# Linear attention with its gate terms made early and kept in DRAM, its halves pipelined in software, the second values projection moved last, and the first scores' operands loaded by another queue

## The chip, the cores and the metric

The kernel runs on one core of one Trainium2 chip. The metric is the device time of one execution in microseconds (us). The engines are named as in the profile: PE is the matmul engine, PEld its weight loads, DVE the vector engine, ACT the scalar engine, POOL the GpSimd engine, SP the engine that here only issues DMAs. A queue named SPq or ACTq is the stream of DMA issues on that engine.

## What is computed

One encoder block for 1024 tokens of width 1024. The part that the change touches is the pair of token mixers, fed by one projection of `x`:

```python
proj = h @ w_in[l]
aq, ak, av, iq, ik, iw, bq, bk, bv, br, bg = jnp.split(proj, split_points, axis=-1)
ya = dsa_mixer(aq, ak, av, iq, ik, iw)          # index scores -> top 256 keys per query -> softmax attention
log_a = log_sigmoid(bg @ w_gla_gate + b_gla_gate) / 16
ob = gla_mixer(bq, bk, bv, log_a)               # chunks of 64 tokens
```
and within `gla_mixer`
```python
b = jnp.cumsum(log_a, axis=2)                   # inside a chunk
qg = qf * jnp.exp(b);  kg = kf * jnp.exp(-b)
A = where(causal, qg @ kg.T, 0);  o_intra = A @ v
kd = kf * jnp.exp(b_last - b);  kv = kd.T @ v;  decay = exp(b_last)
S_next = decay * S + kv;  o_inter = qg @ S_prev
```
Then `mix = [ya | yb] @ w_out`, a layer norm, a mixture of 32 experts with two chosen per token, and a second layer norm.

## The kernel before

`run` opens with `in_phase`: index projections (`index_queries`, `index_keys`), half of the first values projection (`values(0, ...)`), then `index_scores`, which for six query tiles of 128 rows makes eight score products each and, between them, draws steps from a generator `rest`. `rest_inputs` (line 448) makes that generator: first the second values projection, `values(1, ...)`, then `gla_inputs`, which for each of two head pairs projects queries and keys, values, and the output gate of the linear attention and stores them in DRAM (`d_gqk`, `d_gv`, `d_gr`). What is left of `rest` runs after the scores. Then come `queries_keys` (the attention's queries and keys, four weight pieces, rotated by DVE and POOL, stored to `d_q` and `d_k`), `topk_phase` (a threshold search bit by bit over 31 bits, by counting on DVE for four row tiles and on ACT for two, then a tail of six tiles that makes the bias), and `gla_phase` with high priority.

`gla_phase` loops over two head pairs and two halves of the tokens. `gla_half` (line 540) loads its operands, makes the gate terms (lines 553 to 572: four matmuls, a log-sigmoid out of Exp and Ln on ACT, four cumulative-sum matmuls, two Exp), then `kd` by transposes, the masked products, the chunk states `S` one after the other on DVE, the outputs, their norm, and four transposes for each head whose copy `ym` is stored to `d_mix`.

The `attention` works through 32 items, four head pairs by eight query tiles, in an order written out by hand on PE, ACT and DVE (`manual_schedule`). Everything before it is ordered by the framework's planner, which fixes each engine's stream ahead of time: an engine runs its stream in order and stands at an instruction whose operand is not there. `attention_loads(0, ...)` (line 328) loads the operands of the first head pair into the pool `first_qk`, which takes the memory of the linear attention's pool; its values go into a buffer of the pool `big`, whose buffers hold the split `x` while projections run. Inside the attention, `rb` (line 875), the spread reciprocals of the softmax sums, is made by POOL and read by PE in `shares`; `split_wout` (line 904) also works on POOL.

After the attention come the output projection (line 997), the router and the experts (line 1208), whose weights stream in by DMA.

## Time and profile before

| | |
|---|---|
| median of 3 runs | 1330.31 us (1326.86 to 1330.82) |
| the profiled execution | 1329.53 us |
| its span, first to last instruction | 1327.7 us |
| PE busy over the span | 92% |
| DVE, ACT, POOL busy | 78%, 61%, 29% |

The profiled execution lies 0.8 us under the median. Its 1.8 us outside the span are what surrounds the first and last instruction. The busy shares are means over stages that have different limits: up to 124 us the index scores, from there to 392 us the top-k search beside projections and linear attention, to 415 us the last projections, from 428 to 554 us the attention, then the output projection and the router, and from 700 us the experts.

### The profile page before, as it was taken

The numbers are of one execution on the slowest core, as the hardware profiler recorded it, in microseconds if no ns is written. First come the engines' busy times: TensorE is split into PE (matmuls) and PEld (weight loads), VectorE is DVE, ScalarE is ACT, GpSimd is POOL, SyncE is SP. The second block draws the span as 40 slices with busy tenths as digits, with TensorE's granted clock in tenths as the row PEclk, the third lists the DMA queues.
The fourth block names the chain that finished last, engine by engine and source line by source line (L and its number), as shares of the span: only waits on it lengthen the run. The fifth ranks groups of instructions, "written<-read, shape, count | busy, mean of one in ns | idle before, by whom it ended". The sixth has DMA issues, their size and how long they took to land.

```text
span 1327.7 us, 19294 instructions
## 1 busy us (share of the span) xinstructions
PE 1219.5 (92%) x6894; PEld 1013.7 (76%) x6894; DVE 1032.4 (78%) x1647; ACT 803.9 (61%) x1120; POOL 385.3 (29%) x340
## 2 busy tenths in 40 slices
PE   6999999999886899999959999999999999999952
PEld 5986987987665778778857888888888888888741
DVE  4378799899882556467677899999999999998945
ACT  4366577676321666422146777787777787777735
POOL 2412633234763245011120222122112222212014
PEclk9999999999898999999969999999999999999985
DMA  7643334223325793387366999999999999999926
GB/s 251 169 127 114 120 97 134 97 82 106 100 65 176 227 268 96 117 311 273 124 218 257 361 364 378 380 376 361 372 362 369 352 363 357 346 355 343 331 40 253
DMA packets 127652, 318.51 MB, mean 240 GB/s; under 512 B 15353, under 2 KB 45842, under 8 KB 127554
## 3 DMA queue, kind: packets, MB, share of 16 engines
q1 hardware_dynamic: 114754, 287.86, 61.3%
q0 software_dynamic: 10496, 21.00, 6.1%
q10 hardware_dynamic: 2304, 8.39, 1.6%
q8 instruction: 55, 0.90, 0.3%
q14 instruction: 43, 0.35, 0.1%
HBM read 281.74 MB, written 52.23 MB: 252 GB/s over the span
## 4 chain that ended last, share of the span: by engine, by line
PE 63%; DMA 12%; DVE 12%; ACT 5%; issue 4%; POOL 2%; SPq 1%; POOLq 0%; ACTq 0%; DVEq 0%
PE acc L1208 24%; PE ot L1208 11%; PE acc L997 6%; PE acc L235 4%; DMA big<-we 3%; PE acc L221 3%; DVE gt L689 3%; PE pt L1271 3%; DMA d_y<-y,tok 2%; PE s L795 2%; PE ot L833 2%; PE pt L819 2%; PE g L235 2%; DMA d_mix<-ym 1%; ACT jnk L719 1%
## 5 line engine op out<-in xcount | busy, mean ns | idle before, releaser
L180 DVE TENSOR_TENSOR elo<-big,ehi 128x2048 fp32r<-128x2048 f32 (+1 forms) x132 | 268.2, 2060 | 24.6 <-ACT ehi L179 22.1
L179 ACT CAST ehi<-big 128x2048 fp32r<-128x2048 f32 (+1 forms) x132 | 223.3, 1725 | 7.8 <-DMA big<-we 3.6
L1208 PE MATMUL acc<-ehi,xh 128*128 128x512 f32 x512 | 206.4, 403 | 2.0 <-ACT sg L1320 2.0
L1208 PE MATMUL acc<-ehi,xl 128*128 128x512 f32 x512 | 203.4, 397 | 2.5 <-DVE xl L180 2.5
L1208 PE MATMUL acc<-elo,xh 128*128 128x512 f32 x512 | 203.1, 397 | 1.2 <-DVE elo L180 1.2
L221 PE MATMUL acc<-big,whi 128*128 128x512 f32 (+1 forms) x432 | 137.5, 398 | 11.3 <-ACT big L179 10.8
L1278 POOL DMA_INDIRECT xg<-d_h,tok x32 | 37.0, 1157 | 366.8 <-PE pt L1271 366.0
L235 PE MATMUL acc<-whi,big 128*128 128x256 f32 x640 | 120.6, 287 | 0.0
L1257 POOL DMA_INDIRECT d_y<-y,tok x32 | 89.3, 2792 | 106.1 <-DVE y L1256 45.9
L1208 PEld LDWEIGHTS acc<-ehi,xl 128*128 128x128 f32 x512 | 97.0, 189 | 26.2 <-DVE xl L180 3.2
L1208 PEld LDWEIGHTS acc<-ehi,xh 128*128 128x128 f32 x512 | 97.2, 190 | 24.1 <-ACT sg L1320 2.5
L1208 PEld LDWEIGHTS acc<-elo,xh 128*128 128x128 f32 x512 | 97.3, 190 | 23.0 <-DVE elo L180 1.6
L221 PEld LDWEIGHTS acc<-big,whi 128*128 128x128 f32 x432 | 82.9, 196 | 29.2 <-ACT big L179 10.8
L1208 PE MATMUL ot<-ehi,ah 128*128 128x512 f32 x256 | 103.6, 405 | 0.9 <-ACT ah L179 0.9
L689 DVE TENSOR_SCALAR_CACHE_REDUCE gt<-sc,cand 128x384 bf16<-128x384 f32 (+1 forms) x124 | 100.4, 809 | 4.1 <-POOL sc L701 1.6
L180 DVE TENSOR_TENSOR elo<-slot,ehi 128x2048 fp32r<-128x2048 f32 (+1 forms) x46 | 95.5, 2100 | 9.5 <-ACT ehi L179 9.1
L235 PEld LDWEIGHTS acc<-whi,big 128*128 128x128 f32 x640 | 101.1, 192 | 1.8 <-issue 1.0
L1208 PE MATMUL ot<-ehi,al 128*128 128x512 f32 x256 | 101.1, 395 | 0.8 <-DVE al L180 0.8
L1208 PE MATMUL ot<-elo,ah 128*128 128x512 f32 x256 | 101.0, 394 | 0.0
L235 PE MATMUL acc<-wlo,big 128*128 128x256 f32 x320 | 91.9, 288 | 0.0
L719 ACT ACTIVATE jnk<-sc,cand 128x896 bf16<-128x896 f32 (+1 forms) x62 | 67.9, 1095 | 35.4 <-DVE cand L715 26.9
L997 PE MATMUL acc<-wohi,m 128*128 128x512 f32 x256 | 83.8, 402 | 2.4 <-ACT m L179 2.4
(287 smaller groups left out, 2616.7 us busy)
## 6 DMA issues: line engine op xcount, KB each, us to landing
big<-we SPq DMA_DIRECT2D x79, 1024.0 KB
big<-wf SPq DMA_DIRECT2D x40, 1024.0 KB
slot<-we SPq DMA_DIRECT2D x26, 1024.0 KB
sc<-we SPq DMA_DIRECT2D x20, 1024.0 KB
slot<-wf SPq DMA_DIRECT2D x16, 1024.0 KB
wraw<-wi SPq DMA_DIRECT2D x52, 256.0 KB
sc<-wf SPq DMA_DIRECT2D x8, 1024.0 KB
raw<-xT SPq DMA_DIRECT2D x8, 512.0 KB
```

Source lines behind the costliest of these rows:

```text
L179: nc.scalar.copy(hi, src)
L180: (lo_eng or nc.vector).tensor_tensor(lo, src, hi.bitcast(F32), op=OP.subtract)
L221: nc.tensor.matmul(ps[:m, :n], l[:, j, c0:c0 + m], r[:, j % 2, t0:t0 + n], start=(j == 0 and a == 0), stop=(j == 7 and a == 2))
L235: nc.tensor.matmul(ps[:, i, :], l[:, j % 2, s], r[:, j, :], start=(j == 0 and a == 0), stop=(j == 7 and a == 2))
L689: nc.vector.tensor_scalar(gtt[:, :WS[i]], x, v, 0.0, op0=op, op1=OP.add, accum_out=cnt[:, i:i + 1])
L719: nc.scalar.activation(jnk[:, :WS[i]], y[i], AF.Sign, bias=c, accum_out=cnt[:, i:i + 1])
L795: nc.tensor.matmul(ps[:, 512 * c:512 * c + mm], lq, kk[hd][:, a, c0:c0 + mm], start=a == 0, stop=a == 1)
L997: nc.tensor.matmul(ps, l[:, j, :], w[:, j, s], start=(j == 0 and a == 0), stop=(j == 7 and a == 2))
L1208: nc.tensor.matmul(o, x[:, jj, :], w[:, j, s], start=(jj == 0 and a == 0), stop=(jj == n - 1 and a == 2))
L1257: nc.gpsimd.indirect_dma_start(out=self.d_y, out_offset=bass.IndirectOffsetOnAxis(ap=tok.bitcast(U32), axis=0), in_=y, in_offset=None, bou ...
L1271: self.last_mm = nc.tensor.transpose(pt[:, 128 * i:128 * i + 128], src[:, 128 * (b + i):128 * (b + i) + 128], self.c["ident"])
L1278: self.last_gather = nc.gpsimd.indirect_dma_start(out=xg, out_offset=None, in_=self.d_h, in_offset=bass.IndirectOffsetOnAxis(ap=tok.bitcas ...
```

## The change

- The gate terms leave `gla_half` and move into a new function `decays`, called before the index scores. It makes all four halves' terms at once, with the four Exp, then the four Ln, then the eight Exp together, and stores them to DRAM (`d_decay`). The gate's raw input stays in SBUF (`self.bg`) and no longer goes through DRAM (`d_bg`). The scale of 1/16 moves from the matrix `tri` into the last Exp.
- `gla_half` is cut in two. `gla_front` loads a half's operands and its gate terms and makes `qg`, `kg` and `kd`; `gla_phase` calls the next half's front before the rest of this half.
- `rest` holds the six projections of the linear attention only. `values(1, ...)` is called after `topk_phase`.
- The first head pair's operands are loaded from the ACT queue, and their values into a tile of `first_qk`.
- In the tail of `topk_phase` a DVE comparison and an ACT copy with a sum become one ACT Sign with a sum; the equality test reads its 16-bit result.
- In `attention`, the reciprocals and `rb` are made an iteration earlier.

```diff
@@ run
-                    loads = [self.attention_loads(0, [fq.tile([128, 2, D], F32R, name=f"kq{i}") for i in range(3)] + [self.big()])]
+                    loads = [self.attention_loads(0, [fq.tile([128, 2, D], F32R if i < 3 else F32, name=f"kq{i}") for i in range(4)], nc.scalar)]
@@ in_phase
                     self.index_keys(p, w_c, 0, cI, sI)
+                    self.decays(p)
                     self.all_of(self.values(0, w_v, (0, 2)))
-                    rest = self.rest_inputs(gg)
+                    rest = chain(*(self.gla_inputs(gg, hp, k) for hp in range(2) for k in range(3)))
...
                 self.queries_keys(p)
                 self.topk_phase(tp)
+                self.all_of(self.values(1, self.load_w(I["wi"][P_AV + 1], 256), (0, 2, 4, 6)))
@@ new
+    def decays(self, p):
+        wg = p.tile([128, 256], F32, name="wg")
+        nc.sync.dma_start(wg[64:81], self.I["wg"])
+        halves = [(hp, h) for h in range(2) for hp in range(2)]
+        for hp, h in halves:
+            ps = self.bank("g", [128, 512])
+            for i in range(4):
+                t = 4 * h + i
+                nc.tensor.matmul(ps[:, 128 * i:128 * i + 128], self.bg[64:81, t * 128:(t + 1) * 128],
+                                 wg[64:81, 128 * hp:128 * hp + 128], start=True, stop=True)
+            u = p.tile([128, 512], F32, name="u", bufs=4)
+            loga = p.tile([128, 512], F32, name="loga", bufs=4)
+            nc.vector.tensor_scalar(loga, ps, 0.0, None, op0=OP.min)
+            nc.vector.scalar_tensor_tensor(u, loga, 2.0, ps, op0=OP.mult, op1=OP.subtract)
+            nc.scalar.activation(u, u, AF.Exp)
+            logs.append((u, loga))
+        for u, loga in logs:
+            nc.scalar.activation(u, u, AF.Ln, bias=1.0)
+            nc.gpsimd.tensor_tensor(loga, loga, u, op=OP.subtract)
+        for (hp, h), (u, loga) in zip(halves, logs):
+            bp = self.bank("g", [128, 512])
+            for i in range(4):
+                nc.tensor.matmul(bp[:, 128 * i:128 * i + 128], loga[:, 128 * i:128 * i + 128], self.c["causal"],
+                                 start=True, stop=True)
+            for k, tag in enumerate(("u", "loga")):
+                e = p.tile([128, 512], F32, name=f"e{k}", tag=tag, bufs=4)
+                nc.scalar.activation(e, bp, AF.Exp, scale=(0.0625, -0.0625)[k])
+                nc.sync.dma_start(self.d_decay[hp][h][k], e)
@@ gla_phase
+        halves = [(hp, h) for hp in range(2) for h in range(2)]
+        st = self.gla_front(p, *halves[0])
+        for n, (hp, h) in enumerate(halves):
+            this, st = st, self.gla_front(p, *halves[n + 1]) if n < 3 else None
+            S = self.gla_half(p, hp, h, S if h else None, this, AT, causal)
@@ gla_front (what is new in it)
+        eb = p.tile([128, 512], F32, name="eb")
+        en = p.tile([128, 512], F32, name="en")
+        v = p.tile([128, 4, 256], F32, name="v", bufs=2)
+        nc.sync.dma_start(eb, self.d_decay[hp][h][0])
+        nc.sync.dma_start(en, self.d_decay[hp][h][1])
+        kd = p.tile([128, 4, 128], F32, name="kd", bufs=2)
@@ topk_phase, for each of six tiles
-            nc.vector.tensor_scalar(gt, y[i], sg[:, i:i + 1], v[:, i:i + 1], op0=OP.mult, op1=OP.is_gt)
-            nc.vector.tensor_scalar(eq, y[i], sg[:, i:i + 1], v[:, i:i + 1], op0=OP.mult, op1=OP.is_equal)
-            nc.scalar.activation(jnk[:, :W], gt, AF.Copy, accum_out=cnt[:, i:i + 1])
+            nc.scalar.activation(sn, y[i], AF.Sign, scale=sg[:, i:i + 1], bias=v[:, i:i + 1], accum_out=cnt[:, i:i + 1])
+            nc.vector.tensor_scalar(eq, sn, 0.0, None, op0=OP.is_equal)
             nc.vector.tensor_tensor_scan(pre, eq, eq, 0.0, op0=OP.add, op1=OP.max)
-            nc.vector.tensor_scalar(need[:, i:i + 1], cnt[:, i:i + 1], -1.0, float(TOPK), op0=OP.mult, op1=OP.add)
+            nc.vector.tensor_scalar(need[:, i:i + 1], cnt[:, i:i + 1], -0.5, TOPK - 0.5 * W, op0=OP.mult, op1=OP.add)
+            nc.vector.scalar_tensor_tensor(need[:, i:i + 1], pre[:, W - 1:W], 0.5, need[:, i:i + 1], op0=OP.mult, op1=OP.add)
@@ attention
+                    if s["t"] % 4 == 3:
+                        rb = s["rb"] = p.tile([128, 8, 64], F32, name="rb", bufs=2)
+                        rr = p.tile([128, 8], F32, name="rr", bufs=2)
+                        nc.vector.reciprocal(rr, s["rec"].rearrange("p a b -> p (a b)"))
+                        nc.gpsimd.tensor_copy(rb, rr.unsqueeze(2).to_broadcast([128, 8, 64]))
...
-                if done:
-                    rb = done["rb"] = p.tile([128, 8, 64], F32, name="rb", bufs=2)
```

## Rows read from the trace of the kernel before

**Rows 1.** Busy time of each engine in a stretch of 20 us in the experts' stage. Columns: stretch, length, busy us and instruction count of PE, PEld, DVE, ACT and POOL, granted PE clock as a share of full speed, share of the DMA engines, GB/s.

```profile
820.00:840.00 20.00, 20.00 (x94) 16.31 (x93) 18.47 (x12) 15.29 (x13) 4.19 (x2) 1.00 1.03 367
```

**Rows 2.** The same columns in stretches of 10 us, around the start of the index scores, in the tail of the top-k search, and around the start of the attention.

```profile
50.00:60.00 10.00, 10.00 (x73) 9.27 (x72) 4.77 (x7) 2.60 (x6) 7.52 (x7) 1.00 0.57 166
60.00:70.00 10.00, 6.74 (x57) 6.40 (x56) 1.38 (x3) 3.33 (x6) 3.72 (x3) 1.00 0.89 230
70.00:80.00 10.00, 9.99 (x62) 9.76 (x63) 7.36 (x11) 6.82 (x15) 1.57 (x2) 0.83 0.50 136
...
340.00:350.00 10.00, 7.11 (x30) 5.39 (x29) 9.77 (x12) 2.98 (x7) 7.72 (x7) 0.84 0.33 109
...
380.00:390.00 10.00, 7.40 (x33) 5.45 (x34) 9.86 (x11) 5.12 (x20) 5.05 (x5) 0.83 0.20 58
...
420.00:430.00 10.00, 1.82 (x8) 1.70 (x9) 0.78 (x5) 2.53 (x8) 2.52 (x2) 0.50 0.75 253
430.00:440.00 10.00, 9.71 (x69) 7.77 (x69) 6.57 (x19) 6.95 (x19) 0.00 (x0) 0.90 0.71 212
...
460.00:470.00 10.00, 7.17 (x48) 5.19 (x45) 3.96 (x11) 4.27 (x11) 4.69 (x6) 0.83 1.06 282
```

**Rows 3.** PE's instructions in order of time from the end of the projections to the attention. Columns: start us, us, engine, line, operation, tiles and shapes, count, and in brackets the idle time before it and what ended it.

```profile
414.38 0.39 PE L221 MATMUL acc<-big,wlo 128*128 128x512 f32 x1
417.29 0.35 PE L795 MATMUL s<-kq,kq 128*128 128x256 f32 x1 [2.52 <-DMA kq<-d_k]
418.21 0.38 PE L795 MATMUL s<-kq,kq 128*128 128x256 f32 x1 [0.56 <-DMA kq<-d_k]
418.87 0.55 PE L795 MATMUL s<-kq,kq 128*128 128x256 f32 x1 [0.28 <-DMA kq<-d_k]
428.18 0.98 PE L795 MATMUL s<-kq,kq 128*128 128x256 f32 x3 [8.76 <-DMA kq<-d_k]
```

**Rows 4.** The chain of work that ended last, in order of time, from 398 us to 428 us. Columns: start us, us, what.

```profile
398.54 7.99 DMA d_mix<-ym
...
406.62 0.59 ACT ym L644
407.23 7.20 DMA d_mix<-ym
414.45 4.28 DMA kq<-d_k
...
419.45 2.05 SPq L772
...
421.55 2.13 SPq L765
...
423.73 1.00 SPq L768
...
424.78 3.38 DMA kq<-d_k
```

**Rows 5.** The linear attention's last eight transposes on PE, in order of time.

```profile
395.49 0.60 PE L642 MATMUL g<-K,y 128*128 128x128 f32 x4
...
400.97 0.60 PE L642 MATMUL g<-K,y 128*128 128x128 f32 x4
```

**Rows 6.** A DMA issue on the ACT queue, in order of time on that engine.

```profile
590.34 0.33 ACTq L1008 DMA_DIRECT2D d_h<-r  x1
```

**Rows 7.** PE in order of time, without a wait: from the first line of a fence to its last, three products of a values projection (first fence) and of a query and key projection (second) are started.

```profile
250.05 0.40 PE L235 MATMUL acc<-whi,big 128*128 128x256 f32 x2
...
250.41 0.40 PE L235 MATMUL acc<-whi,big 128*128 128x256 f32 x2
```

```profile
390.27 0.39 PE L221 MATMUL acc<-big,wlo 128*128 128x512 f32 x1
...
390.95 0.39 PE L221 MATMUL acc<-big,wlo 128*128 128x512 f32 x1
```

**Rows 8.** PE's groups of instructions from 340 to 390 us. Columns: line, engine, operation, tiles, shapes, count, busy us, mean ns, idle time before the group and what ended it.

```profile
L221 PE MATMUL acc<-big,whi 128*128 128x512 f32 x71 | 25.9, 445 | 0.0
L221 PE MATMUL acc<-big,wlo 128*128 128x512 f32 x36 | 16.2, 450 | 0.0
L628 PE MATMUL g<-S,qg 64*64 64x128 f32 x32 | 3.6, 305 | 3.6 <-DVE S L617 3.6
L601 PE MATMUL g<-v,kd 64*64 64x128 f32 x32 | 2.2, 275 | 2.2 <-DVE need L747 1.8 <-ACT kv L605 0.4
L582 PE MATMUL g<-K,kdT 128*128 128x128 f32 x4 | 0.7, 287 | 2.9 <-POOL kdT L578 2.9
```

**Rows 9.** DVE's groups from 119.5 to 392 us, the same columns: the tail's comparisons and the gate terms. Under them, in order of time, the instruction that makes the last bias.

```profile
L744 DVE TENSOR_SCALAR eq<-sc,sg,v 128x384 bf16<-128x384 f32 (+5 forms) x6 | 6.5, 1077 | 0.0
L743 DVE TENSOR_SCALAR gt<-sc,sg,v 128x384 bf16<-128x384 f32 (+5 forms) x6 | 6.1, 1015 | 0.0
L560 DVE TENSOR_SCALAR loga<-g 128x512 f32<-128x512 f32 x4 | 2.8, 688 | 2.2 <-PE g L556 2.2
L561 DVE SCALAR_TENSOR_TENSOR u<-loga,g 128x512 f32<-128x512 f32 x4 | 2.7, 681 | 0.0
```

```profile
391.40 0.43 DVE L750 TENSOR_SCALAR sc<-gt 128x1024 bf16<-128x1024 bf16 x1 [1.06 <-POOL gt L749]
```

**Rows 10.** The chain of a half's gate terms, from PE's, ACT's and POOL's instructions in order of time.

```profile
314.42 1.15 PE L556 MATMUL g<-wg,bgT 17*128 17x128 f32 x8
...
327.78 1.16 PE L567 MATMUL g<-Kin,loga 128*128 128x128 f32 x8 [1.32 <-POOL loga L564]
```

```profile
321.38 1.28 ACT L562 ACT_TABLE_LOAD   x1
322.67 0.63 ACT L562 ACTIVATE u<-u 128x512 f32<-128x512 f32 x1
```

```profile
326.46 1.27 POOL L564 TENSOR_TENSOR loga<-loga,u 128x512 f32<-128x512 f32 x1 [11.94 <-DVE gt L689]
```

**Rows 11.** PE's first index scores, in order of time, with the wait ahead of them.

```profile
70.01 1.73 PE L479 MATMUL acc<-K,Q 128*128 128x384 f32 x5 [3.27 <-DMA K<-dk]
```

**Rows 12.** The one long wait of PE inside the attention, and POOL's work ahead of it, in order of time.

```profile
464.79 0.66 PE L841 MATMUL pt<-K,rb 128*128 128x128 f32 x4 [2.83 <-POOL rb L878]
```

```profile
461.10 2.50 POOL L909 TENSOR_TENSOR wolo<-woraw,wohi 128x512 fp32r<-128x512 f32 x2
...
464.11 0.62 POOL L878 COPY rb<-rr 128x512 f32<-128x512 f32 x1
```

More of the change, by code (lines that the diff above doesn't have):

```diff
@@ L1 @@
 from contextlib import ExitStack, nullcontext
+from itertools import chain
 import numpy as np
@@ L306, in run @@
             self.sc = mp.tile([128, SOFF[-1]], F32, name="sc")
-            self.d_bg = self.dram.tile([16, T], F32, name="d_bg")
+            self.d_decay = [[self.dram.tile([2, 128, 512], F32, name=f"d_decay{hp}{h}") for h in range(2)] for hp in range(2)]
             scb = self.sc.bitcast(BF)
@@ L439, in index_keys @@
         nc.scalar.copy(self.iwT[32:40, q0 - IQ0:t0 + 512 - IQ0], cps[32:40, q0 - t0:])
-        bg = p.tile([128, 512], F32, name="bg")
-        nc.scalar.copy(bg[64:80], cps[64:80, :])
-        nc.sync.dma_start(self.d_bg[:, ts], bg[64:80])
+        nc.scalar.copy(self.bg[64:80, ts], cps[64:80, :])
         r = self.rope(p, 16, 512, cps[0:16, :], cps[96:112, :], (cI[0:16, ts], cI[96:112, ts]),
@@ L446, in index_keys @@
             self.split_out(p, r[i], dk[i, :, ts], dk[2 + i, :, ts], nc.vector)
-    def rest_inputs(self, gg):
-        yield from self.values(1, self.load_w(self.I["wi"][P_AV + 1], 256), (0, 2, 4, 6))
-        yield from self.gla_inputs(gg)
     def index_scores(self, p, rest):
@@ L496, in rstd, with gla_inputs @@
         self.last_pow = nc.gpsimd.tensor_tensor(out, out, self.mhalf[:, :n], op=OP.pow)
-    def gla_inputs(self, gg):
+    def gla_inputs(self, gg, hp, k):
         nc, I = self.nc, self.I
-        for hp in range(2):
-            w = self.load_w(I["wi"][P_GLA + 3 * hp], 256)
+        w = self.load_w(I["wi"][P_GLA + 3 * hp + k], 256)
+        if k == 0:
             for h in range(2):
@@ L514, in gla_inputs @@
                 nc.sync.dma_start(self.d_gv[hp][:, t:t + 2], o)
-            w = self.load_w(I["wi"][P_GLA + 3 * hp + 2], 256)
+        else:
             for t in range(0, NT, 2):
@@ L558, in gla_half @@
-        u = p.tile([128, 512], F32, name="u", tag="u")
-        loga = p.tile([128, 512], F32, name="loga")
-        nc.vector.tensor_scalar(loga, ps, 0.0, None, op0=OP.min)
-        nc.vector.scalar_tensor_tensor(u, loga, 2.0, ps, op0=OP.mult, op1=OP.subtract)
-        nc.scalar.activation(u, u, AF.Exp)
-        nc.scalar.activation(u, u, AF.Ln, bias=1.0)
-        nc.gpsimd.tensor_tensor(loga, loga, u, op=OP.subtract)
-        bp = self.bank("g", [128, 512])
-        for i in range(4):
-            nc.tensor.matmul(bp[:, 128 * i:128 * i + 128], loga[:, 128 * i:128 * i + 128], self.c["tri"],
-                             start=True, stop=True)
@@ L635, in gla_half @@
             self.rstd(ss, ss, 1.0 / 128)
-            y = p.tile([128, 4, 128], F32, name="y", tag="kdT")
+            y = p.tile([128, 4, 128], F32, name="y")
             for i in range(4):
```

80 lines of the change are left out of this document (33 added, 47 removed).

## The prediction

> **What bounds the kernel now.** I read the stages from the back. In the experts PE is busy for the whole of such a stretch at full clock, 94 products in 20 us [rows 1], and every expert waits for the router, which waits for the attention. So a microsecond by which the attention ends earlier reaches the end whole, and the question is when the attention starts and how long it runs. Next I read PE in order of time at the seam in front of it [rows 3]. The last projection ends at 414.8 us. Three score products squeeze through, and the attention really begins at 428.18 us, after a wait of 8.76 us for operands. The chain of waits [rows 4] says why those are late. The linear attention's last two results share one buffer, `ym`: the first store takes 7.99 us, only then can the second copy run, its store takes 7.20 us, and the operand tile that takes over this memory is loaded at 414.45 us, on the very end of it. Then the SP queue itself is the chain: its issues of L772, L765 and L768 take 2.05, 2.13 and 1.00 us. In front of the seam I read the busy table in small stretches [rows 2]. PE looks busy but does little between 340 and 390 us: DVE is full there (9.77 and 9.86 of 10 us in the outer two stretches), PE stands before linear-attention products, and its granted clock drops to 0.83 and 0.84, which means that part of those stretches ran at 1.2 instead of 2.4 GHz.
>
> **The seam (the load queue, the place of the values projection).** The second values projection is four banks of 48 products. Three products in sequence start 0.36 us apart [rows 7], so it costs 192 x 0.12 = 23 us of PE. Its removal from the front brings all that follows on PE forward by up to 23 us: the linear attention's inputs, and with them its last transposes, which now stand at 395.5 and 401.0 us [rows 5]. The cut gate chain and the early front bring them forward further. At the end the 23 us come back, as work that needs none of what the attention waits for. So the stores of `ym` and the operand loads get some 23 us of cover that they don't have now. The sixteen load issues move from SP, where they stand behind stores of queries and keys, to ACT; one issue on ACT took 0.33 us [rows 6], so sixteen are 5 us of an ACT that is idle for most of 390 to 425 us. If they go one by one at SP's long durations of 2 us they are some 30 us. Behind them on ACT stand the copies that empty the values' banks and the first softmax exponentials; in front of them may stand the last Sign of the top-k tail. The gap is 428.2 - 414.8 = 13.4 us, less 1.1 us of products inside it: 12.3 us to win, 0 at worst by this mechanism. I take **11**, as the cover is longer than the two stores together. After the gap PE runs at the low level: 0.50 in 420 to 430 and 0.90 in 430 to 440 [rows 2], that is half of the 1.8 us left in the first and a tenth of the second, 1.9 us lost; without a gap it stays up. I take **1.5**, bounds 0 and 1.9. The values' tile no longer needs a `big` buffer, which is what lets this load pass in front of the last projection.
>
> The Trainium skill, DMA: Bandwidth & Descriptors, section Issuing engines are not separate DMA queues, speaks against this part: the queues share the same DMA engines, so that a second issuing engine saves issue time only. By that rule the operands still come when memory and stores let them. That is the first rival below. The trace of before can't decide it, since there issue and stores both stand on the chain.
>
> **The tail of the projections.** From 340 to 390 us PE did 107 products of 512 columns [rows 8]. At the 0.227 us apart at which they follow when nothing stops them, three in 0.68 us [rows 7], these are 24.3 us. The linear attention's groups, by their places in the order of time some 10 us, make it 34 of 50. So 16 us are lost to waits for DVE and POOL (3.6, 2.2 and 2.9 us of idle in the three groups shown) and to the slower clock. After the change the linear attention passes earlier, away from the tail of the top-k search, its `kd` is made a half ahead, and the planner has the values projection, which needs only ACT, to put beside DVE's rush. But the planner fixes the order ahead and saw no such waits before either. Bounds: 16, and below nothing at -5 if the early halves meet DVE's counting loop instead, which is nearly as full. I take half, **8**.
>
> **DVE and the top-k search.** It doesn't set the end: the last bias is made at 391.8 us [rows 9], 23 us before the last projection. DVE loses the gate terms in that window, 2.8 + 2.7 = 5.5 us, and the tail's comparison, 6.1 us [rows 9]; the equality test on 16-bit data costs between nothing and its 6.5 us of now; six short operations are added at under 0.2 us. So the search ends some 10 to 15 us sooner if it starts when it does now. In the tail the Sign on ACT now stands in line ahead of the equality test, where the ACT sum used to run beside the scan; at about 1 us by six tiles that gives 6 us back. All this is hidden as long as the last bias comes before the start of the attention, at 404 to 415 us: **0**, cover at least 15 us.
>
> **The gate terms made early.** PE's share is the same before and after, only its place changes: four halves of 1.15 us (L556) and 1.16 us (L567) [rows 10], 9.2 us. What can cost is the chain in front of the index scores, since it holds both `g` banks that these also use: matmuls 1.1, two DVE operations 1.4, table load and Exp 1.9, load and Ln 1.9, POOL 1.3, matmuls 1.1, load and Exp 1.9 us [rows 9, 10] (Ln and the last Exp priced as the first), 10.6 us for the first half, with ACT's further 3 Exp, 3 Ln and 7 Exp at 0.6 us behind it. ACT is busy for 2.60, 3.33 and 6.82 us of the three stretches from 50 to 80 us, and PE waits 3.27 us for the keys before the first score [rows 2, 11], so much of it finds room; DVE is nearly idle there as well. Bounds: -10, nothing hidden, and +2, the wait filled. PE's order matters more than the scores' start, since a late search still has its 15 us of cover. I take **-2**. The eight stores and the eight loads, 256 KB each, replace nothing big; the DMA engines' share is under 0.9 in these stretches and the loads can go a half ahead: 0, and if they come late PE waits in the pipelined halves, which the -5 above holds.
>
> **The reciprocals in the attention.** One iteration earlier `rb` leaves its place behind the two subtractions of 2.50 us on POOL [rows 12]. PE's wait of 2.83 us goes, and with it the fall of the clock to 0.83 in 460 to 470 us [rows 2], 1.7 us. DVE now waits for the sums an iteration sooner, eight times, under 0.5 us each where it is not idle anyway. Bounds 0 and 4.5; I take **4**.
>
> **Sum.** 11 + 1.5 + 8 + 0 - 2 + 4 = 22.5 us. From the profiled execution's 1329.5 us that gives 1307.0 us; the median of the runs lies 0.8 us higher, so the same sum from there gives 1307.8.
>
> **The rivals.**
> *The operands stay late.* The loads still begin only after the last store of `ym`, because their memory is the linear attention's, or ACT comes to the issues late behind its copies. Then about 12 us of gap remain, now after the values projection: 11 and 1.5 are gone, 1319.5 us. For it: the chain [rows 4] runs through the store, not through the queue alone. Against: the linear attention has 23 us more in hand.
> *The tail is not filled.* Queries and keys stay pinned to DVE's rotations, which stand behind the search, so that the last of them ends near 405 us as now less 10, and the values projection follows as 23 us of bare tail to 428 us. The gap is gone but nothing else: the start stays at 428, and only the reciprocals and the clock are won, 1324 us. For it: DVE is full to 390 us [rows 2]. Against: PE needs DVE only to free six banks.
> *Slower: ACT stands at a load.* The planner puts the ACT issues ahead of Signs of the top-k tail. ACT then stands at a load until a store of 7 to 8 us has landed, the tail's six tiles stand behind it and the values' copies too, so that the start moves from 428 to 440 us: 1329.5 + 12 - 4 = 1337 us. It decides from the point at which ACT's wait passes the 15 us of cover and the 13 us of the old gap together. Against it: ACT's stream has room, and no such chain stands there now.
>
> **How the numbers follow.** Forecast 67%, operands late 14%, tail not filled 10%, slower 9%. A difference of 0.3%, 4 us, is about what a measurement of this kernel can tell from none. The forecast's own range is 22.5 with the ends of its terms: at best 12.3 + 1.9 + 16 + 4.5 = 34.7, 1295 us; at worst about 10, where not all go wrong at once, 1319 us. The range must take in the first two rivals, so 1295 to 1325 us, with the slower case and a tenth at the ends left out. Faster: 65 of the forecast, 12 of the first rival, 6 of the second, 83%; the same 8%; slower 9%.
>
> **What would show it.** In the profile after: PE's last projection is a values product (L235's place), and the first scores follow within 2 us, with the load issues on ACTq before it; the linear attention's last transposes before 375 us; PE's product count between 340 and 390 us up and its granted clock at 1.0; the last bias before 392 us; the index scores' start no later than 73 us; no wait of PE for `rb`. The prediction is wrong if a wait of PE for operands of the first scores is still over 5 us, if the scores start much after 75 us, or if the start of the attention lies behind 420 us.

## The result, and the profile after

The changed kernel takes 1342.2 us (median of 4 runs, 1340.8 to 1346.2) where before takes 1329.9 us beside it: ratio 1.0101, interval 1.0074 to 1.0129. It is slower by 1%; 1307 us was forecast, with a range from 1295 to 1325. The profiled execution's span is 1339.0 us, against 1327.7.

The difference can be laid out by four marks on PE, each read from a line's first and last start, before and after: first product with the values 432.2 and 430.2 us, last transposes of the attention's shares 553.6 and 547.9, first product of the output projection 555.1 and 566.2, end of the span. So the attention starts 2.0 us earlier, runs 3.7 us shorter (121.4 and 117.7), then PE stands 16.8 us longer, and the rest is the same (772.6 and 772.8): -2.0 - 3.7 + 16.8 + 0.2 = 11.3 us. The work up to the attention's start gave almost nothing, and a wait that the prediction doesn't have cost more than all that was won.

The same stretches as in [rows 2], after:

```profile
70.00:80.00 10.00, 3.72 (x20) 3.20 (x18) 0.00 (x0) 9.90 (x14) 3.53 (x3) 0.72 0.18 64
...
380.00:390.00 10.00, 10.00 (x71) 9.38 (x70) 7.30 (x9) 1.20 (x3) 4.36 (x4) 1.00 0.67 222
420.00:430.00 10.00, 3.23 (x12) 2.48 (x12) 1.35 (x8) 4.53 (x13) 0.00 (x0) 0.50 1.01 262
```

The tail of the projections has PE at full clock now, as forecast; the index scores' start has lost PE, and the seam is as empty as before. PE at the seam, after, in order of time (start, us, engine, line, operation, tiles, shapes, count, and in brackets the idle time before it and what ended it):

```profile
406.46 0.39 PE L817 MATMUL s<-kq,kq 128*128 128x256 f32 x2
418.03 1.22 PE L817 MATMUL s<-kq,kq 128*128 128x256 f32 x4 [11.17 <-ACT vs L674]
424.54 0.48 PE L841 MATMUL pt<-K,Sm 128*128 128x128 f32 x1 [5.29 <-ACT Sm L830]
...
429.59 0.66 PE L841 MATMUL pt<-K,Sm 128*128 128x128 f32 x2 [2.23 <-DVE PT L844]
430.18 0.70 PE L855 MATMUL ot<-PT,kq 128*64 128x128 f32 x4
```

Against [rows 3]: the first scores do follow the last projection at once (406.46 us), and no wait of theirs for operands is left. But the next three waits, 18.7 us together, name ACT twice. ACT in the same stretch:

```profile
403.49 1.24 ACT L764 ACTIVATE sn<-sc,v,sg 128x1024 bf16<-128x1024 f32 x1 [7.44 <-DVE sc L772]
...
405.77 1.06 ACT L674 COPY vs<-acc 128x512 f32<-128x512 f32 x2
417.39 0.59 ACT L674 COPY vs<-acc 128x512 f32<-128x512 f32 x1 [10.57 <-DMA d_av<-vs]
422.09 0.59 ACT L674 COPY vs<-acc 128x512 f32<-128x512 f32 x1 [4.11 <-DMA d_av<-vs]
422.70 1.28 ACT L830 ACT_TABLE_LOAD   x1
423.99 0.40 ACT L830 ACTIVATE Sm<-Sm,mx 128x128 f32<-128x128 f32 x1
```

The first exponential (L830) stands, in order, behind four copies of the last values. They have two buffers, `vs`; the third and fourth copy wait for the stores of the first two. The chain of waits, after, gives those stores' price (start, us, what):

```profile
405.42 3.26 POOL rp L180
...
409.31 0.55 SPq L675
...
410.60 11.40 DMA d_av<-vs
```

SP issues the first of them at 409.31, 3.5 us after the copy began, since stores of keys that wait for POOL's split stand ahead. Now the end of the attention, on PE, and the loads of W_out on POOL, first in before and then after:

```profile
553.25 0.66 PE L841 MATMUL pt<-K,rb 128*128 128x128 f32 x4
555.10 0.50 PE L997 MATMUL acc<-wohi,m 128*128 128x512 f32 x1 [1.19 <-ACT m L179]
```

```profile
451.50 1.43 POOL L901 DMA_DIRECT2D woraw<-wo  x2 [8.68 <-DMA big<-d_k]
```

```profile
547.50 0.66 PE L863 MATMUL pt<-K,rb 128*128 128x128 f32 x4
566.16 0.80 PE L1019 MATMUL acc<-wohi,m 128*128 128x512 f32 x1 [18.00 <-ACT m L179]
```

```profile
482.73 0.61 POOL L888 COPY rb<-rr 128x512 f32<-128x512 f32 x1 [16.43 <-DVE rr L887]
489.47 1.42 POOL L923 DMA_DIRECT2D woraw<-wo  x2 [6.12 <-DMA big<-d_k]
```

POOL issues the first load of W_out (the weights of the output projection) at 489.47 us; in before it was 451.5. The last product that reads the values tile in `first_qk` starts at 488.9. So the splitting of W_out starts 38 us later and ends at 564 us (532 in before). The mixed heads, which are loaded into W_out's buffers, come after that, and PE waits 18.0 us.

### The profile page after: what moved, and what is told of

Its sections match the earlier page's. It is cut to its first block, busy times and chain, and to the rows that moved or that the text cites. A ratio compares the mean times of both kernels' runs of the same rounds, so it can differ in the third digit from the quotient of the medians.

```text
span 1339.0 us, 19330 instructions
## 1 busy us (share of the span) xinstructions
PE 1218.8 (91%) x6894; PEld 1011.5 (76%) x6894; DVE 1016.0 (76%) x1646; ACT 801.1 (60%) x1117; POOL 385.5 (29%) x340
## 4 chain that ended last, share of the span: by engine, by line
PE 67%; DMA 13%; DVE 9%; ACT 4%; issue 3%; POOL 2%; SPq 0%; ACTq 0%; POOLq 0%; DVEq 0%
PE acc L1230 23%; PE ot L1230 11%; PE acc L1019 7%; PE acc L235 6%; PE acc L221 4%; DVE eq L709 3%; PE pt L1293 3%; PE s L817 3%; PE ot L855 2%; DMA d_y<-y,tok 2%; PE pt L841 2%; DMA slot<-we 2%; PE g L221 2%; DMA big<-wf 2%; PE ot L1046 1%
## 5 line engine op out<-in xcount | busy, mean ns | idle before, releaser
L235 PE MATMUL acc<-whi,big 128*128 128x256 f32 x736 | 136.5, 285 | 0.4 <-ACT rel L478 0.4
L221 PE MATMUL acc<-big,whi 128*128 128x512 f32 (+1 forms) x384 | 120.8, 394 | 9.7 <-ACT big L179 9.7
L1279 POOL DMA_INDIRECT d_y<-y,tok x32 | 92.8, 2900 | 100.5 <-DVE y L1278 40.6
L235 PEld LDWEIGHTS acc<-whi,big 128*128 128x128 f32 x736 | 115.4, 191 | 2.4 <-issue 0.9
L1230 PEld LDWEIGHTS acc<-elo,xh 128*128 128x128 f32 x512 | 97.3, 190 | 22.5 <-DVE elo L180 1.2
L709 DVE TENSOR_SCALAR_CACHE_REDUCE eq<-sc,cand 128x384 bf16<-128x384 f32 (+1 forms) x124 | 100.5, 810 | 5.9 <-POOL sc L721 3.4
L235 PE MATMUL acc<-wlo,big 128*128 128x256 f32 x368 | 104.7, 285 | 0.0
L739 ACT ACTIVATE sn<-sc,cand 128x896 bf16<-128x896 f32 (+1 forms) x62 | 67.9, 1095 | 48.5 <-DVE cand L735 46.2
L221 PEld LDWEIGHTS acc<-big,whi 128*128 128x128 f32 x384 | 73.0, 194 | 25.5 <-ACT big L179 9.7
```

The source lines that it names most:

```text
L221: nc.tensor.matmul(ps[:m, :n], l[:, j, c0:c0 + m], r[:, j % 2, t0:t0 + n], start=(j == 0 and a == 0), stop=(j == 7 and a == 2))
L235: nc.tensor.matmul(ps[:, i, :], l[:, j % 2, s], r[:, j, :], start=(j == 0 and a == 0), stop=(j == 7 and a == 2))
L709: nc.vector.tensor_scalar(gtt[:, :WS[i]], x, v, 0.0, op0=op, op1=OP.add, accum_out=cnt[:, i:i + 1])
L739: nc.scalar.activation(jnk[:, :WS[i]], y[i], AF.Sign, bias=c, accum_out=cnt[:, i:i + 1])
L1230: nc.tensor.matmul(o, x[:, jj, :], w[:, j, s], start=(jj == 0 and a == 0), stop=(jj == n - 1 and a == 2))
L1279: nc.gpsimd.indirect_dma_start(out=self.d_y, out_offset=bass.IndirectOffsetOnAxis(ap=tok.bitcast(U32), axis=0), in_=y, in_offset=None, bou ...
```

## The experiments

Ratios are to before, with 95% intervals.

**1. The values tile back in `big`.**

```
-  [fq.tile(..., F32R if i < 3 else F32, name=f"kq{i}") for i in range(4)], nc.scalar)
+  [fq.tile(..., F32R, name=f"kq{i}") for i in range(3)] + [self.big()], nc.scalar)
```

> The changed kernel with one part undone: the values tile of the first head pairs goes back to a `big` buffer. Everything else as after. Theory W (its place in first_qk keeps that memory until the last product with it, at 488.9 us, so the W_out tiles that take the memory over load from 489 and not from 451 us, and PE stands before the output projection): the first W_out load is back near 450 us, PE's wait of 18.0 us behind the attention falls to some 9 us or less, the time falls by 9 to 17 us, to 1325 to 1333. Rival S (the loss is all in the late search and the seam; the late W_out splits only show where the attention is late anyway): 1340 to 1343, and the wait of 18 us stays within 3. Rival B (the tile in `big` waits for the linear attention's last store, and ACT, in order, stands at that load): W_out is early but the attention starts 5 us or more later than 424 to 430 us, and the time stays above 1335.

1328.6 us, ratio 0.9986 (0.9973 to 0.9999): 13.6 us less than after. POOL and PE of this kernel:

```profile
453.31 1.41 POOL L923 DMA_DIRECT2D woraw<-wo  x2 [15.29 <-PE s L817]
```

```profile
550.65 0.66 PE L863 MATMUL pt<-K,rb 128*128 128x128 f32 x4
...
552.50 0.50 PE L1019 MATMUL acc<-wohi,m 128*128 128x512 f32 x1 [1.19 <-ACT m L179]
```

**2. The same place put into the kernel before** (the reverse edit, loads by SP).

> The kernel before with one part of the change alone: the values tile of the first head pairs in first_qk, as the changed kernel has it; loads by SP as before. Theory W: W_out loads from about 490 us, PE's wait behind the attention grows from 9 us to 18 or more: before + 9 to + 17 us, less what the first scores win since the values load no longer waits for the last `ym` store (0 to 5 us): 1334 to 1345. Rival S: 1326 to 1331, not later than before.

1346.0 us, 1.0122 (1.0104 to 1.0140), 1 us over the range of theory W. PE waits 18.4 us before the output projection (L997), and the first load of W_out is released by a product with the values:

```profile
495.99 1.43 POOL L901 DMA_DIRECT2D woraw<-wo  x2 [0.71 <-PE ot L833]
```

```profile
573.04 0.80 PE L997 MATMUL acc<-wohi,m 128*128 128x512 f32 x1 [18.37 <-ACT m L179]
```

Both directions agree: theory W is shown, 14 to 15 us.

**3. Gate terms in table order,** in the changed kernel: issue edges put the four Exp ahead of the four Ln, and these ahead of the last Exp.

```
+  with self.tc.issue_after(last.ins):
       ln = nc.scalar.activation(u, u, AF.Ln, bias=1.0)
...
+  with self.tc.issue_after(ln.ins):
       nc.scalar.activation(e, bp, AF.Exp, scale=(0.0625, -0.0625)[k])
```

> The changed kernel with ACT's gate terms in table order: all four Exp, then all four Ln, then the eight last Exp, where the planner had put Exp and Ln alternately (8 table loads of 1.28 us between 62 and 75 us). Theory G (the alternation holds up the gate chain, that the `g` banks and PE, that the index scores, that the top-k search, and the search's end at 413 us the start of the attention): 2 or 3 table loads, the last score sum 4 to 9 us before 137.4, the last bias as much before 413.2, the start of the attention and the time 4 to 9 us earlier: 1333 to 1338. Rival V (the seam is held by the stores of the values' copies and ACT's order, not by the search): the search is earlier but the attention not by more than 2 us: 1340 to 1342.

1344.6 us, 1.0113 (1.0093 to 1.0134): nothing gained.

**4. The same with the values tile in `big`** (edits 1 and 3):

> Both: the values tile in `big` and the gate terms in table order. Theories W and G together: 1342 less 9 to 17 less 4 to 9 = 1316 to 1329, a few us under the kernel before. If W holds and the seam is held by something else than the search: as with the tile in `big` alone, within 2 us. If neither: 1340 to 1342.

1331.6 us, 1.0008 (0.9999 to 1.0017), nothing over experiment 1. In the fourth two tables are loaded for Ln and the last Exp, and the last score sum starts at 137.4 us, 4.9 us sooner (after: 142.3, the figure that expectation 3 should have had), but the search ends at 351.1 (after: 352.1) and its tail takes longer, last bias 420.8 (after: 413.2). Theory G falls as an account of the time: scores that come earlier did not bring the attention forward. Whether the search's end follows the scores is mixed: here it doesn't; in experiment 11 below it does (last rectification of a score 7.0 us sooner than in experiment 1, search's end 6.9).

**5. Four buffers for the last values,** on experiment 1 (values tile in `big`):

```
-  vs = self.wpool.tile([128, 2, 2, 128], F32, name="vs", bufs=2)
+  vs = pool.tile(..., name="vl", bufs=2) if pool and t > 2 else self.wpool.tile(..., name="vs", bufs=2)
```

> The version with the values tile back in `big` (1328.6 us), and in it four instead of two buffers for the last values projection's copies, so that no copy waits for a store. Theory V (the seam is held by ACT: the first softmax exponentials stand behind the third and fourth copy, which wait 11.1 and 4.7 us for the stores of the first two): those two waits go, the first exponential comes 8 to 14 us before 425.2, and the first product with values, 432.1 us, 6 to 12 us earlier: 1317 to 1323. Rival M (the memory of the copies is taken over by the attention's PT tiles, so that the last store holds the start anyway): exponentials earlier, the first product with values no more than 4 us: 1325 to 1329. Rival S (the late end of the search, last bias at 413.3 us, holds it): 1326 to 1329.

1318.6 us, 0.9911 (0.9880 to 0.9943): 10 us, theory V. The first exponential comes at 416.6 instead of 425.2. Rival M is the next holder, as the chain of waits shows:

```profile
403.73 4.51 POOL rp L180 x2
...
409.14 12.89 DMA d_av<-vs
...
422.15 0.30 DVE PT L844
```

**6. Gate terms late,** on experiment 1: `decays` and its DRAM tiles out, the same operations back in `gla_front`.

```
-  self.decays(p)
...
+  nc.scalar.activation(u, u, AF.Exp)
+  nc.scalar.activation(u, u, AF.Ln, bias=1.0)
+  nc.gpsimd.tensor_tensor(loga, loga, u, op=OP.subtract)
```

> The version with the values tile in `big`, and in it the gate terms again where before had them, in the linear attention's halves, not early and not through DRAM (for room in memory `y` shares the buffer of `kdT` again, the sums S have three buffers and the gate inputs come by halves). The halves stay software-pipelined. Theory G (the early terms are what delays index scores and search): the first score at 65 to 71 us with no wait of PE near 78, the last score sum near 125 to 130, the last bias 12 to 20 us before 413.3. On the end: if V holds too, the stores of the last values still hold ACT, so 1322 to 1328. Rival S (search alone holds the seam): 1313 to 1319.

1352.6 us, 1.0152 (1.0105 to 1.0200).

**8. The same on experiment 5:**

> The version with the values tile in `big`, with both: gate terms late as before had them, and four buffers for the last values' copies. Theories G and V together (two delays in one place, each hidden by the other): the start of the attention near 412 to 420 us instead of 432, the time 1308 to 1318. If only V holds: as with the buffers alone. If the start is held by the stores and the operand loads themselves (memory taken over): 1322 to 1329.

1349.9 us, 1.0155 (1.0113 to 1.0197). None of the theories saw it. Of experiment 6, the scores' rectification and the end of the search, by line (shortest, median and longest in ns, first and last start in us):

```profile
L477 ACT ACTIVATE rel<-acc x80: 432/540/645, 69.9 to 126.0; 128x384 f32<-128x384 f32 x24, 128x512 f32<-128x512 f32 x24, 128x320 f32<-128x320 f32 x16, 128x448 f32<-128x448 f32 x16
...
L742 DVE SCALAR_TENSOR_TENSOR v<-thr,sg x1: 166/166/166, 351.1 to 351.1; 128x6 f32<-128x6 f32 x1
```

The scores are early again (last 126.0; after 140.0) and the search still ends at 351.1 (after: 352.1). This speaks against G too, less cleanly, since the gate terms are back inside the search. What moves is the linear attention: its last transposes run at 424.2 us (after: 361.9), among the last projections, which end at 428. The three changes for room in memory are in this too, so the 24 to 31 us aren't the gate terms' alone.

**7. First loads on SP,** on experiment 1:

```
-  ... + [self.big()], nc.scalar)
+  ... + [self.big()])
```

> The version with the values tile in `big`, and in it the first loads of queries and keys back on SP instead of ACT. Theory L (ACT stands at load issues in front of the tail's Signs, 7 us, and so delays the search's end and the start): last bias 5 to 8 us before 413.3 and the time 5 to 8 us lower: 1321 to 1324. If V holds the seam, the search's end moves and the time does not: 1326 to 1330. If the queue was what a gain hung on (issues by SP late at 1 to 2 us each): the start later by 5 us or more, 1333 or more.

1325.3 us, 0.9965 (0.9947 to 0.9983); the interval overlaps that of experiment 1.

**10. The same on experiment 5:**

> The version with the values tile in `big` and four buffers for the last values' copies (1318.6 us), and in it the first loads of queries and keys on SP again. If the ACT queue costs the 3 us that it cost with two buffers (1328.6 against 1325.3): 1315 to 1316. If with free copies ACT has nothing behind the issues any more: 1318 to 1320. If the ACT queue is what brings the operands in time now: 1322 or more, and PE waits for kq operands at the seam.

1319.0 us, 0.9901 (0.9881 to 0.9921), nothing.

**13. The same on experiment 12** (further down):

> The version with four buffers and the values' stores on ACT (1313.2 us), and in it the first loads of queries, keys and values on SP again. There ACT stands 7.5 us at the issue of the values load (its memory was the activations', free when the last projection ends), with the fourth copy and the first exponentials behind it; the load itself then lands at 419.7 us, after 13.1 us. Theory A (ACT's stand at the load holds the start): exponentials from 415 to some 408 us, the start from 419.7 to 413 to 416, 1308 to 1311. Theory T (the transfer of the values tile holds it, whoever issues it): exponentials earlier, the first product with values within 2 us of 419.7, 1312 to 1315. Rival Q (SP issues it behind its stores of keys, which wait for POOL): later than 422, 1316 or more.

1317.9 us, 0.9908 (0.9883 to 0.9934). With these loads on SP instead of ACT the time changes by -3, 0 and +5 us; the queue gives no steady gain of its own. The +5 isn't all the queue's: of the 4.3 us by which the first product with values is later than in experiment 12 (424.0 against 419.7), 3.2 are there at the search's end (352.5 against 349.3), ahead of the first of these loads.

**9. The reciprocals early, alone in before** (the change's lines of `attention`).

> The kernel before with one part of the change alone: the reciprocals and their copy `rb` an iteration earlier. The prediction's own term: 4 us, bounds 0 and 4.5, so 1326 to 1327, PE's wait for `rb` near 464 us gone. If the wait only moves to the next thing that is late (PT copies, ACT): 1329 to 1331.

1332.2 us, 1.0015 (1.0000 to 1.0029): nothing gained. The wait for `rb` is gone and another stands later on PE:

```profile
489.89 0.90 PE L819 MATMUL pt<-K,Sm 128*128 128x128 f32 x3 [4.43 <-ACT R L843]
```

ACT's copy of `R` there waits 6.3 us for the store of an earlier `R`.

**11. The values projection in its old place,** on experiment 1:

```
-  self.all_of(self.values(1, self.load_w(I["wi"][P_AV + 1], 256), (0, 2, 4, 6)))
...
+  rest = chain(self.values(1, ..., (0, 2, 4, 6)), *(self.gla_inputs(...) ...))
```

> The version with the values tile in `big` (1328.6 us), and in it the second values projection in its old place, in front of the linear attention's inputs. Everything else as there. By the prediction's reasons (23 us of PE as cover at the seam, linear attention 23 us earlier) the place at the end is worth 10 to 20 us: 1338 to 1350. By theory V (at the end it puts ACT's waits for its stores in front of the first exponentials, 16 us): the two cancel, 1326 to 1332. By theory D (DVE's total work up to the last bias is what counts and the order only deals it out): last bias some 15 to 20 us before 413, the time within 4 us.

1327.7 us, 0.9978 (0.9961 to 0.9995). The place is worth nothing with two buffers: the last projection ends 2 us earlier (first score 406.0 against 407.9), the start is the same (431.9 and 432.1); with the projection at the front the exponentials stand on ACT behind a cast of keys that waits 9.4 us for a store. Theory D falls, as the last bias moves by 3 us only. The place at the front was not tried together with the edits of experiments 5 and 12.

**12. The last values' stores issued by ACT,** on experiment 5:

```
-  nc.sync.dma_start(self.d_av[g][:, :, t:t + 2, :]..., vs)
+  (nc.scalar if pool else nc.sync).dma_start(self.d_av[g][:, :, t:t + 2, :]..., vs)
```

> The version with four buffers (1318.6 us), and in it the four stores of the last values issued by ACT behind each copy instead of by SP, where they stand behind the last stores of keys, which wait for POOL (issue at 409.1 us, copy done at 404.7). Theory P (PT's memory is the copies' memory; the first transposes to be copied wait for the last store, which ends at 422.0): stores 3 to 4 us earlier, the start from 423.2 to 418 to 420: 1314 to 1316. Rival B (the stores share the DMA engines with keys and operand loads, 0.8 to 0.9 busy there, and only take longer): 1317 to 1320. Rival A (the store issues, in order on ACT, delay the exponentials): 1320 to 1323.

1313.2 us, 0.9861 (0.9840 to 0.9882), the fastest. The time is as theory P has it, the mechanism only in part: from first score to first product with values it is 16.1 us, against 16.9 in experiment 5. The other 2.7 us of the earlier start are projections that end earlier (403.6 against 406.3), and those are there already at the last rectification of a score (139.3 against 142.3), in a stage that the edit doesn't touch. In that stage the two executions differ in PE's granted clock, 0.50 in experiment 5 (first line) and 0.81 in experiment 12:

```profile
80.00:90.00 10.00, 9.05 (x30) 7.34 (x30) 4.62 (x8) 7.02 (x16) 3.74 (x4) 0.50 0.82 267
```

```profile
80.00:90.00 10.00, 9.30 (x42) 7.71 (x43) 5.13 (x8) 7.03 (x15) 3.43 (x3) 0.81 0.83 269
```

So about half of the 5.4 us may be this difference and not the stores' issue; why the clock differs isn't found. The chain of waits in experiment 12:

```profile
405.44 1.02 ACTq L675
...
406.56 13.12 DMA big<-d_av
...
419.73 0.69 PE ot L855 x4
```

Now the load of the values tile holds the start: its memory, a buffer of the split `x`, is free only when the projections end.

**14. The second pair's loads later,** on experiment 12 (`if n in (3, 12, 19)` for `(0, 12, 19)`).

> The version with four buffers and the values' stores on ACT (1313.2 us), and in it the loads of the second head pair's queries and keys three tiles later (at the fourth score tile, not at the first). Theory T with contention (the values load of 1 MB takes 13.1 us because the second head pair's 1.5 MB and the values' stores run beside it): it lands 3 to 5 us sooner, the start 415 to 417, 1309 to 1311, as long as the second pair's scores do not wait. If contention is not what makes it slow: 1312 to 1315. If the second pair comes late: a wait of PE near 435 us, 1316 or more.

1315.2 us, 0.9883 (0.9854 to 0.9912), no difference. SP issues the first of these loads at 411.24 us, 3.2 us after the first score (experiment 12: 407.06, 3.5 us after), so that it hardly tried what it meant to; contention stays open.

**15. Gate terms early, alone in before,** halves not pipelined.

> The kernel before with one part of the change alone: gate terms early, kept in DRAM and loaded by the halves, which are not pipelined. The prediction's term: -2 us (a loss), bounds -10 and +2, and half of the 8 us of the tail in its favour. Theory G (the early chain holds up scores and search, 13 to 20 us, DVE's order does the rest): last bias 10 us or more after 391, but the last projection earlier than 414.8; the attention starts with the later of them and the operands: 1326 to 1334. If the cut chain in the halves is what brings the linear attention forward (the late gate terms made 1350 of 1319 in the other arrangement): the last projection before 408 us and 1318 to 1325. If neither: 1329 to 1333.

1328.6 us, 0.9994 (0.9977 to 1.0010). The projections end at 408.5 instead of 414.8 us, the last bias comes at 408.9, and a values load of 14.2 us, issued at 420, holds the start at 434.2.

**16. Halves not pipelined,** on experiment 12 (`this = self.gla_front(p, hp, h)` in the loop).

> The version with four buffers and the values' stores on ACT (1313.2 us), and in it the halves of the linear attention not pipelined: each half makes its own operands directly ahead of itself. If the pipelining is what lets the linear attention pass early: its last transposes later than now, the projections' end at 408 or later, 1317 to 1325. If the early gate terms alone do it and the last values fill PE: 1312 to 1315.

1323.9 us, 0.9959 (0.9939 to 0.9979): 10.8 us lost. The projections end at 418.4 us (403.5) and the last bias comes at 423.4 (408.6). The last transposes of the linear attention are not later, though (347.5, against 359.0): what the pipelining frees is the time of the other work, not that mark.

**17. The first pair's values in a small pool of their own,** on the changed kernel with four buffers and stores by ACT:

```
+  vvp = outw.enter_context(self.pool("vv0", side="right"))
...
+  [fq.tile(...) for i in range(3)] + [vvp.tile([128, D], F32, name="vv0")]
```

> The changed kernel with the first head pair's half of the values tile in a small pool of its own (4 KB a partition), neither in first_qk, where W_out's memory waits for it, nor in `big`, which is free only when the last projection ends; the second pair's half in `big`, loaded with that pair. Four buffers for the last values' copies, their stores on ACT. Theory T (in the 1313.2 us version the load of the values tile, 13.1 us after the projections' end, holds the start at 419.7): the load lands before the projections end, and the start comes 4 to 8 us sooner, held by the exponentials and by PT's memory: 1305 to 1309, with W_out early as before. Rival C (the stores of the copies, whose memory PT takes over, hold it at the same place): 1312 to 1315. Rival A (ACT stands at the early loads in the top-k tail, in front of the copies and exponentials): 1314 to 1320.

1322.9 us, 0.9940 (0.9921 to 0.9958).

**18. The same with the loads on SP.**

> The same with the first loads on SP. Theory T with ACT's stands of some 7 us in the tail gone: 1303 to 1308. If SP comes to them behind its stores of keys (POOL's splits): the first scores wait, 1314 or more. If the queue matters to nothing: within 2 us of the version with ACT.

1321.6 us, 0.9930 (0.9911 to 0.9949). W_out stays early (PE's output projection starts 1.5 us after the attention) and the values tile is there, yet the start is later than in experiment 12 (419.7), at 431.3 and 428.6, and the time of experiment 17 is above all three ranges given for it. ACT of experiment 17:

```profile
411.21 0.59 ACT L675 COPY vl<-acc 128x512 f32<-128x512 f32 x1 [0.75 <-PE s L818]
425.91 0.37 ACTq L676 DMA_DIRECT2D d_av<-vl  x1
426.31 1.28 ACT L831 ACT_TABLE_LOAD   x1 [14.51 <-DMA d_k<-rp]
```

It is of rival C's kind, with another store: that of the last keys, 14.6 us long by the chain, ends the wait of ACT.

## Why the prediction was wrong, step by step

Of the 33.8 us between the forecast's gain of 22.5 us and the loss of 11.3, 16.8 are the wait for W_out and 18.8 the seam (12.5 forecast, -6.3 measured); the other terms nearly cancel.

**The term put at nothing: the memory of the values' tile.** "The values' tile no longer needs a `big` buffer, which is what lets this load pass in front of the last projection" was costed at nothing. The tile is read until the second head pair's last tile, and the memory that it moved into is what W_out's tiles take over. That costs 13.6 us taken out of after and 15.2 us put into before. None of the rivals has it; with the slower case at 9% the chances were too sure. The work that hid W_out's splitting was in the trace of before, 451 to 532 us, and wasn't named.

**The seam, 11 + 1.5.** The first half of the step holds: 23 us of values products cover the `ym` stores and the operand loads, and the first scores follow within 0.2 us. (The waits of the old gap in [rows 3] add up to 12.1 us, not 12.3.) The step that fails is "the cover is longer than the two stores together": the cover issues stores of its own. From the first score to the first product with values it is 23.7 us, where before took 17.4 from the last projection: 6.3 us lost. The copies were named as standing behind the load issues, but priced as if they never wait. Two buffers make 10 us (experiments 1 and 5), and with them a projection at the end is worth nothing (experiment 11). The low clock stays too, 0.50 in 420 to 430 us.

The first rival (operands late) was right that the memory is the point: in the versions with four buffers, except experiments 8 and 16, a DMA that takes 9 to 15 us and starts between 406 and 416 us ends the wait. It is the copies' store in experiment 5, the values load in 10, 12, 13 and 14, and the last keys' store in 17 and 18. From first score to first product with values it is 16 to 17 us in experiments 5, 10, 12, 13 and 14. What moved the start in the fastest version is that the projections end earlier: 419.7 against 432.2, 12.5 us, of which 11.2 are the projections (403.6 against 414.8), some 3 us of them perhaps by the granted clock (see experiment 12).

Experiments 7, 10 and 13 agree with the rule of the Trainium skill cited above (DMA: Bandwidth & Descriptors, Issuing engines are not separate DMA queues): changing the issuing engine gave no steady gain (-3, 0 and +5 us).

**The tail of the projections, 8.** Right: 414.8 to 406.5 us, 8.3. The marks given for it are there too: the linear attention's last transposes at 361.9 us, the clock at 1.00 from 380 to 390 us, a values product last. Its size was in part luck, as it was taken as half of a bound of 16. Early gate terms alone bring 6 us (experiment 15), and in the fastest version the pipelining is needed for it (experiment 16).

**Gate terms, -2, bounds -10 and +2.** The place was wrong; what it cost at the end isn't shown alone. The first five score products come at 70.63 us, within the "no later than 73" of the text, but the sixth, at 72.61 us in before, only at 79.67, behind the gate chain:

```profile
70.63 1.10 PE L477 MATMUL acc<-K,Q 128*128 128x384 f32 x5
77.97 2.05 PE L547 MATMUL g<-Kin,loga 128*128 128x128 f32 x8 [6.23 <-issue]
79.67 0.67 PE L477 MATMUL acc<-K,Q 128*128 128x384 f32 x1
```

The index weights are ready at 84.8 us instead of 65.2. In the order that the planner gave it, ACT alternates Exp and Ln, and each loads a table:

```profile
61.89 1.28 ACT L542 ACT_TABLE_LOAD   x1
63.19 0.63 ACT L542 ACTIVATE u<-u 128x512 f32<-128x512 f32 x1
63.84 1.28 ACT L539 ACT_TABLE_LOAD   x1
65.13 0.63 ACT L539 ACTIVATE u<-u 128x512 f32<-128x512 f32 x1
65.78 1.28 ACT L542 ACT_TABLE_LOAD   x1
```

These are eight loads up to 76.8 us; the text had priced one chain and then "0.6 us" each. PE is busy for 3.7 us in 70 to 80 us. Putting the tables in order bought nothing (experiments 3 and 4), and early gate terms with what they win in the tail change the time by nothing (experiment 15).

**DVE, 0, with 15 us of cover.** Wrong in sign: the last bias is ready 21.8 us later (413.6 against 391.8), not 10 to 15 sooner. 17.8 us of this are there at the last rectification of a score (140.0 against 122.2) and 3.6 more at the search's end (352.1 against 330.7). Early scores alone don't bring them back: in experiment 6, with the gate terms inside the search again, the last bias is at 412.0. The tail from there to the last bias is as long as in before (61.5 and 61.1 us), though DVE's work in it did fall, from 56.3 to 42.2 us. DVE now waits there, longest for a Sign that stands on ACT behind the last copy `ym`, which waits for a store (ACT, then DVE):

```profile
372.57 0.59 ACT L664 COPY ym<-g 128x512 f32<-128x512 f32 x1 [9.25 <-DMA d_mix<-ym]
373.05 0.92 ACT L764 ACTIVATE sn<-sc,v,sg 128x640 bf16<-128x640 f32 x1
```

```profile
374.10 0.33 DVE L765 TENSOR_SCALAR eq<-sn 128x640 bf16<-128x640 bf16 x1 [7.06 <-ACT sn L764]
```

Whether the late tail does harm isn't settled. In the changed kernel the last Sign (403.49 us, after 7.44 us for DVE) stands on ACT ahead of the last casts of keys and the copies of the values. In experiment 10 the chain of waits runs from the last bias over the first scores to the load of the values:

```profile
412.58 0.43 DVE sc L772
...
413.84 0.80 PE s L817 x2
...
415.32 9.46 DMA big<-d_av
```

In experiment 12 the third score product waits until 409.86 us for DVE's first maxima, which follow the last bias (408.6). No run takes the new form of the tail away alone, so its price stays open.

**The reciprocals, 4.** In the changed kernel the wait is gone and the attention is 3.7 us shorter, but that the reciprocals did it isn't shown. Alone in before they give nothing, since a store of `R` is late next, and in experiment 15, which has them in the old place, the attention is nearly as short (118.5 us; 121.4 in before, 117.7 after).

**The slower rival** gave 1337, near the result, by another mechanism. ACT did stand at the load issues in the search's tail (6.70 us in front of the Sign at 382.32 us, by ACT's instructions in order), but loads on SP save 3 us at most.

## What to carry to other kernels

A tile that is moved to other memory has two prices: when its new memory is free for it, and who waits for that memory until its last reader. Ask both of each tile in a diff, also where no instruction changes. Work moved to a seam as cover brings its copies and stores along; count its buffers against the landing time of one store, and look at what stands in order behind the copies. Where several holders end at nearly the same time, removing one is worth nothing: here the place of the projection gave nothing while its copies waited, and the fastest version (one edit undone, two things mended, 1.4% under before) came from taking the holders one by one.

## What the runs showed of the hardware

A 256 KB store of keys took 9.46 us from issue to landing, 394.65 to 404.1 us in experiment 14, while the DMA engines were busy for 0.29 of the stretch and moved 112 GB/s:

```profile
394.65 9.46 DMA d_k<-so_hi
```

```profile
395.00:404.00 9.00, 9.00 (x77) 9.00 (x76) 6.50 (x8) 1.48 (x3) 5.16 (x4) 1.00 0.29 112
```

So the length of this store isn't a matter of full DMA engines; what it waited for isn't shown. Among the gate terms above a table load of 1.28 us on ACT starts 0.02 us after the activation before it ends, so that a switch cost there its 1.28 us and hardly more.
